# A decoder block: the late modulation products on VectorE, and attention with its TensorE order written out

## The chip, the cores and the metric

One core of one Trainium2 chip runs the whole block. Its engines have a queue each and are tied together by semaphores: TensorE (PE) multiplies matrices into PSUM, VectorE (DVE), ScalarE (ACT) and GpSimd (POOL) do the elementwise work, and DMAs are issued from the queues of SyncE (SP) and ACT. The metric is the device time of one execution in microseconds (us); smaller is better. Of the kernel before three runs were timed, and one more execution was profiled.

## The reference

The input x is 1024 tokens of 1024 channels, with one conditioning vector c. All is float32.

```python
mod = silu(c) @ w_ada + b_ada                    # 6 x 1024: sh1, sc1, g1, sh2, sc2, g2
h = rmsnorm(x, norm1_g) * (1 + sc1) + sh1
u, q, k, v, gate_a, gate_b = split(h @ w_in)     # 512, 512, 512, 512, 1024, 1024
y_a = s5_branch(u, ...) @ w_a                    # 32 groups, 64 complex states each, then a GLU
y_b = stick_breaking_attention(q, k, v) @ w_b    # 8 heads of 64
x = x + g1 * ((sigmoid(gate_a) * y_a + sigmoid(gate_b) * y_b) @ w_o)
h = rmsnorm(x, norm2_g) * (1 + sc2) + sh2
x = x + g2 * ((silu(h @ w_ffn_gate) * (h @ w_ffn_up)) @ w_ffn_down)
out = rmsnorm(x, norm_f_g)
```

Stick-breaking attention gives key j the weight exp(log_sigmoid(z_j) + the sum of log_sigmoid(-z) over the later keys before the query), for keys strictly before the query. So each query needs a running sum over its keys from the latest backwards.

## The kernel before

A scheduler with a timeline of its own sets the order of the instructions on each engine; the program text gives dependencies, buffer counts and a few extra order edges ("pins").

Most products are float32 made of three products of rounded halves: an operand is split into a high half (fp32r, "wh", "pa" first part) and a low half ("wl"), and PE multiplies high x high, high x low, low x high. One projection of 128 output channels is 2 halves of the tokens x 8 slices of channels x 3 = 48 matmuls of 512 columns (`project`, recorded at L619). Its weight is loaded (`weight`, L404), split on ACT or POOL (L411, L413) and DVE or POOL (L414).

The stages, in order: the first modulations and u; the S5 branch in four runs m = 0 to 3 (tables on POOL, scans on DVE, transposes and products on PE, tiles through memory); during it v (`v_proj`) and the first gate (`gate(0, m)`) as filling for PE; then glu, q and k of the first head pair, branch a; then attention; then branch b, the output projection and the feed-forward part.

**The later modulations.** In the S5 stage `ada_rest` makes modulations 4 to 11, two per S5 run: the weight tile `aw` (128 x 2 x 512, 0.5 MB) comes by DMA, PE multiplies it by the conditioning vector into a PSUM bank `adp` (L770, with 32 partitions for every one of four slices), ACT copies the bank to `acc` (L785), and SP stores that (L786). The sum over partitions is made later. The `aw` tiles and `acc` lie in a pool (`ar`) that closes at the end of the S5 stage; tiles of glu (`raw`, loaded at L831) take that place.

**Attention.** There are 4 head pairs, 2 halves Q of the queries, and in each half units of keys: two or one blocks of 128 keys on the diagonal, then one block after the other backwards; 3 units in the first half and 7 in the second, 40 units in all. A unit holds both heads. `scores` makes z = k q on PE (L704) into two PSUM banks, adds the mask on DVE (L712) or copies z (L714), makes log(1 + exp(-|z|)) on ACT (L715 to L717), adds max(z, 0) on DVE (L718), and splits that into halves (high on ACT L719, low on DVE L720). `heads` then subtracts the sums of the units behind it (tile `wb`) on POOL (L737), sums over the keys of the block with triangular ones on PE (L741, PSUM pair `acc`), adds the first row of these sums to the running row on DVE (L750, L752), sends the row to memory (L754) and back to all partitions as the next `wb` (L756), subtracts the sums on DVE (L758), takes exp on ACT (L759), and multiplies by the values on PE (L763). PSUM has eight banks of 512: two pairs for z, one pair for `acc`, one for the values, and one for projections (`mm`).

Beside attention run the projections that nothing in it waits for at once: q and k of the next head pair (`qk_proj`), bound to the scores ten units back, and the eight parts of the second gate (`gate(1, m)`), each bound to one of the scores by the list PINS.

## Time and profile before

| | |
|---|---|
| three timed runs | 1606.18, 1602.16, 1599.55 us; median 1602.16 |
| the profiled execution, its own time | 1606.37 us |
| its span, first to last instruction | 1604.7 us |
| mean granted PE clock | 0.962 |
| S5 stage (v to glu's first matmul) | 101.3 to 316.2 us |
| glu, q and k, branch a | 316.2 to 403.4 us |
| attention (first scores to the start of branch b) | 408.2 to 740.1 us |

In the profile PE is the matmul engine, DVE, ACT and POOL are VectorE, ScalarE and GpSimd; a "q" behind an engine (SPq) means its queue. L and a number is a line of the kernel. A group line gives line, engine, operation, out<-in with sizes, xcount, then busy us, mean ns of one, and the idle time of its engine just before them with what ended most of it. A line of waits gives the total, how many times and the longest. PE matmuls overlap, so the time of one is read from the distance to the next and not from its own length.

### The profile page before, as it was taken

What the parts mean: (1) busy time and instruction counts of PE and PEld (TensorE: products, weight loads), DVE (VectorE), ACT (ScalarE), POOL (GpSimd) and SP (SyncE); (2) the same over time, 40 slices, a digit from 0 to 9 for tenths busy, and PEclk for the clock granted to TensorE, in tenths of its full rate; (3) what the DMA queues carried; (4) which work ended last, traced back from release to release, by engine and by line L of the source; (5) the groups of instructions that cost most, each with busy time, mean ns of one, the idle gap of its engine ahead of it and who ended that gap; (6) DMA issues with size and microseconds to landing.
All of it is one profiled execution on the core that took longest, in us unless ns stands there. A gap on an engine that the chain in (4) does not pass through costs nothing.

```text
span 1604.7 us, 18605 instructions
## 1 busy us (share of the span) xinstructions
PE 1461.0 (91%) x6706; PEld 1118.6 (70%) x6706; DVE 1064.4 (66%) x1269; ACT 640.3 (40%) x824; POOL 768.8 (48%) x602
## 2 busy tenths in 40 slices
...
GB/s 288 157 146 168 170 193 213 157 77 191 79 79 66 119 86 150 71 116 190 151 158 105 129 43 112 109 112 114 116 114 110 64 160 245 146 150 164 99 27 105
DMA packets 180452, 210.48 MB, mean 131 GB/s; under 512 B 28612, under 2 KB 121896, under 8 KB 180360
## 3 DMA queue, kind: packets, MB, share of 16 engines
...
q8 instruction: 53, 0.87, 0.2%
...
## 4 chain that ended last, share of the span: by engine, by line
PE 50%; DVE 19%; POOL 11%; issue 11%; DMA 5%; ACT 4%; SPq 0%; ACTq 0%; DVEq 0%; POOLq 0%
PE tq L1052 10%; PE mm L619 10%; PE wo L1052 8%; PE wo L933 5%; PE ga L619 4%; PE gu L1052 3%; PE mm L578 2%; PE mx L619 2%; PE acc L741 1%; PE z L704 1%; POOL p L71 1%; DVE f L1127 1%; POOL pb L1144 1%; DVE wa L758 1%; DVE x L1140 1%
## 5 line engine op out<-in xcount | busy, mean ns | idle before, releaser
L737 POOL TENSOR_TENSOR wa<-wa,wb 128x1024 f32<-128x1024 f32 (+2 forms) x32 | 68.9, 2153 | 164.3 <-DMA wb<-cD 105.2
L430 POOL TENSOR_TENSOR ws<-wb 128x1024 f32<-128x1024 f32 x29 | 73.3, 2527 | 103.9 <-DVE wl L433 58.4
L430 POOL TENSOR_TENSOR wgs<-wb 128x1024 f32<-128x1024 f32 x15 | 37.0, 2468 | 106.4 <-DVE x L433 37.8
L718 DVE SCALAR_TENSOR_TENSOR ws<-wa,ws 128x1024 f32<-128x1024 f32 (+1 forms) x40 | 56.3, 1411 | 30.1 <-ACT ws L717 30.0
L414 POOL TENSOR_TENSOR wl<-ws,wh 128x1024 fp32r<-128x1024 f32 x10 | 26.3, 2638 | 92.5 <-ACT wh L411 92.5
L1105 POOL TENSOR_TENSOR pa<-pa,row 128x1024 f32<-128x1024 f32 x22 | 64.6, 2957 | 1.9 <-DMA pa<-in_w_ffn_down_dram 1.7
L704 PE MATMUL z<-q,k 64*128 64x512 f32 (+3 forms) x192 | 49.5, 594 | 16.4 <-ACT ws L715 8.0
L758 DVE TENSOR_TENSOR wa<-wa,acc 128x512 f32<-128x512 f32 (+1 forms) x80 | 46.6, 620 | 25.1 <-POOL wa L737 22.9
L1043 POOL TENSOR_TENSOR f<-f,f 128x512 f32<-128x512 f32 x30 | 50.1, 1694 | 27.2 <-DVE f L1033 18.6
L619 PE MATMUL mm<-pa,wgh 128*128 128x512 f32 x176 | 57.8, 409 | 3.7 <-POOL wgh L413 3.4
L619 PE MATMUL mm<-pb,wgh 128*128 128x512 f32 x176 | 57.3, 404 | 1.9 <-ACT gst L657 1.9
L759 ACT ACTIVATE wa<-wa 128x1024 f32<-128x1024 f32 (+1 forms) x40 | 38.8, 970 | 46.0 <-DVE wa L758 46.0
L411 ACT CAST wh<-ws 128x1024 fp32r<-128x1024 f32 x30 | 31.3, 1046 | 62.9 <-PE wo L933 31.2
L413 POOL TENSOR_SCALAR wgh<-wgs 128x1024 fp32r<-128x1024 f32 x8 | 11.5, 1439 | 91.9 <-PE ga L619 59.2
L719 ACT CAST wh<-ws 128x1024 fp32r<-128x1024 f32 (+1 forms) x40 | 38.4, 961 | 42.1 <-DVE ws L718 36.0
L619 PE MATMUL mm<-pa,wh 128*128 128x512 f32 x160 | 51.8, 405 | 0.0
L720 DVE TENSOR_TENSOR wl<-ws,wh 128x1024 fp32r<-128x1024 f32 (+1 forms) x40 | 50.1, 1254 | 2.4 <-ACT wh L719 2.3
L1032 ACT ACTIVATE f<-f 128x1024 f32<-128x1024 f32 x22 | 23.3, 1061 | 62.2 <-DVE f L1072 32.8
L1125 POOL TENSOR_TENSOR wb<-pa 128x512 f32<-128x512 f32 x23 | 40.6, 1776 | 15.7 <-DVE wxl L1123 5.5
L619 PE MATMUL mm<-pb,wh 128*128 128x512 f32 x144 | 45.8, 398 | 1.7 <-ACT q L672 1.7
L741 PE MATMUL acc<-wh,upto 128*128 128x512 f32 (+1 forms) x80 | 34.1, 426 | 13.8 <-DVE wa L758 13.8
L619 PEld LDWEIGHTS mm<-pa,wgh 128*128 128x128 f32 x176 | 34.3, 198 | 17.6 <-POOL wgh L413 5.7
(779 smaller groups left out, 4839.0 us busy)
## 6 DMA issues: line engine op xcount, KB each, us to landing
...
```

The lines of the kernel that those rows point to most:

```text
L430: (add or nc.gpsimd).tensor_tensor(st, a, b, op)
L619: self.nc.tensor.matmul(ps, lhsT=w[a][:, k], rhs=act[h][k][:, b], start=(j == 0), stop=(j == n - 1))
L704: prev = nc.tensor.matmul(z[:, x, f:f + w], lhsT=k[h, P * kb:P * kb + P], rhs=q[h, 512 * Q + c:512 * Q + 512], start=True, stop=True)
L718: nc.vector.scalar_tensor_tensor(st, at, 0.0, st, ALU.max, ALU.add)
L720: nc.vector.tensor_tensor(lt, st, ht.bitcast(F32), ALU.subtract)
L737: nc.gpsimd.tensor_tensor(a[:, :, o], a[:, :, o], behind[:, :, old], ALU.subtract)
L741: nc.tensor.matmul(r[:, x, 0:f], lhsT=self.upto, rhs=parts[n][:, x, 0:f], start=n == 0, stop=n == 1 and behind is not None)
L758: nc.vector.tensor_tensor(a[:, x, 0:f], a[:, x, 0:f], r[:, x, 0:f], ALU.subtract)
L933: nc.tensor.matmul(ps, lhsT=mg[t // 4][k][:, a, P * (t % 4):P * (t % 4) + P], rhs=ws[k // 2][b][:, k % 2], start=(j == 0), stop=(j == 23))
L1043: nc.gpsimd.tensor_tensor(o, a, b, op)
L1052: self.nc.tensor.matmul(ps, lhsT=w[x][:, q, k], rhs=self.B[i](y, k), start=(j == 0), stop=(j == 11))
L1105: nc.gpsimd.tensor_tensor(w, w, g2, ALU.mult)
```

## The change

Two parts.

1. `ada_rest` makes the products on DVE: one multiply and seven multiply-adds of 128 x 512 for each modulation, straight into `acc`. The bank `adp`, PE's products and ACT's copy fall away; the freed bank goes to the projections of that stage (`mx` has 2).

2. Attention is written as one loop over the 40 units in which every PE instruction keeps its program order (`pinned`). At step i come: the sums of unit i, 8 projection matmuls, the values of unit i - 1, the scores of unit i + 3, 8 projection matmuls. The 14 projections (q and k of three head pairs, 8 gates) are one stream of 672 matmuls from a generator, with weights loaded two jobs ahead. PSUM: one pair for z, one pair for `acc`, one bank for the values, three for projections. The copy of z goes from DVE to ACT, the high half from ACT to POOL, the scores' tile `wa` has 5 buffers, and the broadcast row `wb` has 1 where it had 2.

```diff
-ZPB = 2
+ZPB, MXB = 1, 2
-WAB2, WSB, WHB, RWB, CBB = 4, 2, 2, 2, 2
-QPIN = -10
-PINS = (0, 5, 10, 15, 20, 25, 30, 35)
+WAB2, WSB, WHB, RWB, CBB = 5, 2, 2, 2, 1
+LOOK = 3
+FILL = (8, 8, 12)
+JOBS = (("q", 1), ("k", 1), ("g", 0), ("g", 1), ("q", 2), ("k", 2), ("g", 2), ("q", 3), ("k", 3), ("g", 3), ("g", 4), ("g", 5), ("g", 6), ("g", 7))
+AHEAD = 2
...
+    def pinned(self, *args, **kw):
+        return self.tc.keep_in_program_order(self.nc.tensor.matmul(*args, **kw))
+    def fillers(self, qk, qp, kp, gp):
+        nc = self.nc
+        rings = [self.wring[0], self.wring[0], self.wring[2]]
+        jobs = [(n, i) for n, i in JOBS]
+        loaded = []
+        def load(j):
+            n, i = jobs[j]
+            c0 = {"q": 512, "k": 1024, "g": 3072}[n] + P * i
+            loaded.append(self.w3(self.weight(self.in_cols(c0), lo_eng=nc.gpsimd, hi_eng=nc.gpsimd if n == "g" else None, ring=rings[j % 3])))
+        for j in range(AHEAD):
+            load(j)
+        for j, (n, i) in enumerate(jobs):
+            if j + AHEAD < len(jobs):
+                load(j + AHEAD)
...
+            for h in range(2):
+                s = slice(512 * h, 512 * h + 512)
+                ps = self.mm.tile([P, 512], F32, name="mm")
+                c = 0
+                for k in range(KT):
+                    for a, b in PRODUCTS:
+                        self.pinned(ps, lhsT=loaded[j][a][:, k], rhs=self.hT[h][k][:, b], start=c == 0, stop=c == 23)
...
+                        yield
...
     def scores(...)
-            nc.vector.tensor_copy(at, z)
-        nc.scalar.activation(st, at if diag else z, AF.Abs)
+            nc.scalar.copy(a, z)
+        nc.scalar.activation(st, a, AF.Abs)
...
-        nc.scalar.copy(ht, st)
+        nc.gpsimd.tensor_scalar(ht, st, 1.0, 0.0, ALU.mult, ALU.add)
...
+    def attention(self, qk, qp, kp, vp, op, gp, work):
...
+        for i in range(-LOOK, len(units) + 1):
+            if 0 <= i < len(units):
+                self.sums(units[i], work)
+                some(FILL[0])
+            if i > 0:
+                u = units[i - 1]
...
+                self.values(u, ops[u.hp])
+            if i + LOOK < len(units):
+                self.scores(units[i + LOOK], qk, work)
+                some(FILL[1] if i >= 0 else FILL[2])
+        some(10000)
...
-    def ada_rest(self, n, ap, pp, first):
+    def ada_rest(self, n, ap, first):
...
+        acc = ap.tile([P, 512], F32, name="acc", bufs=2)
         for k in range(0, KT, AK):
             w = ap.tile([P, AK, 512], F32, name="aw", bufs=ARB)
             self.after(nc.sync.dma_start(out=w, in_=w_v[:, k:k + AK, 512 * n:512 * n + 512]), first)
-            ws.append(w)
-        ps = pp.tile([P, 512], F32, name="adp")
-        for k in range(KT):
-            self.ada_mm(ps, k, ws[k // AK][:, k % AK])
-        acc = ap.tile([P, 512], F32, name="acc", bufs=2)
-        nc.scalar.copy(acc, ps)
+            for j in range(AK):
+                cj = self.cond[:, k + j:k + j + 1]
+                if k + j == 0:
+                    nc.vector.tensor_scalar(acc, w[:, j], cj, None, ALU.mult)
+                else:
+                    nc.vector.scalar_tensor_tensor(acc, w[:, j], cj, acc, ALU.mult, ALU.add)
         nc.sync.dma_start(out=self.aD[:, n - 4], in_=acc)
```

`sums` and `values` hold what `heads` did behind the scores, in the same form.

The order on the engines, at three places. First DVE in the last S5 run, before (`rt` is a table of S5, `s5s` the injected states, `tc` and `tn` rotations, `scr` scratch, `wl` a weight's low half):

```order
L266 TENSOR_TENSOR rt<-rt,dd 16x8x16
L296 TENSOR_TENSOR scr<-s5s_1786,tc 128x512
L297 TENSOR_TENSOR scr<-s5s_1795,tn 128x512
L298 TENSOR_TENSOR scr<-scr 128x512
L299 TENSOR_TENSOR scr<-s5s_1795,tc 128x512
L300 TENSOR_TENSOR scr<-s5s_1786,tn 128x512
L304 SCALAR_TENSOR_TENSOR scr<-rho,scr 128x128 x4
```

And the same place now (L871 is the new multiply-add):

```order
L871 SCALAR_TENSOR_TENSOR acc<-aw,cond,acc 128x512 x3
L266 TENSOR_TENSOR rt<-rt,dd 16x8x16
L296 TENSOR_TENSOR scr<-s5s_1771,tc 128x512
L871 SCALAR_TENSOR_TENSOR acc<-aw,cond,acc 128x512
L297 TENSOR_TENSOR scr<-s5s_1780,tn 128x512
L871 SCALAR_TENSOR_TENSOR acc<-aw,cond,acc 128x512
L298 TENSOR_TENSOR scr<-scr 128x512
L871 SCALAR_TENSOR_TENSOR acc<-aw,cond,acc 128x512
L299 TENSOR_TENSOR scr<-s5s_1780,tc 128x512
```

The products stand between the steps of S5's chain on the same queue.

Second, SP's queue at the end of S5, before (`yD` is S5's result, `aw` and `aD` the modulations, `raw` glu's input):

```order
L332 DMA yD<-y 16x8x128 x4
L779 DMA aw<-in_w_ada_dram 128x2x512 x2
L658 DMA gD<-gst 128x512
L404 DMA ws<-in_w_glu_dram 128x4x256
L658 DMA gD<-gst 128x512 x2
L786 DMA aD<-acc 128x512
L404 DMA wgs<-in_w_a_dram 128x4x256
L831 DMA raw<-yD 128x512 x2
```

And now:

```order
L872 DMA aD<-acc 128x512
L666 DMA gD<-gst 128x512
L412 DMA ws<-in_w_in_dram 128x8x128
L666 DMA gD<-gst 128x512
L412 DMA wgs<-in_w_in_dram 128x8x128
L412 DMA ws<-in_w_glu_dram 128x4x256
L332 DMA yD<-y 16x8x128 x4
L412 DMA ws<-in_w_glu_dram 128x4x256
L917 DMA raw<-yD 128x512 x2
```

The last modulation is now stored ahead of S5's last result, and the loads of `raw` follow that result.

Third, DVE in attention in a stretch of full units, before (L758 subtracts the sums of one unit, L718 and L720 are the softplus add and low half of a later one):

```order
L720 TENSOR_TENSOR wl_4239<-ws_4237,wh_4238 128x1024
L714 COPY wa_4296<-z_4300 128x1024
L752 TENSOR_TENSOR row_4226<-row_4196,acc_4221 1x1024
L758 TENSOR_TENSOR wa_4206<-wa_4206,acc_4221 128x512 x2
L718 SCALAR_TENSOR_TENSOR ws_4267<-wa_4266,ws_4267 128x1024
L752 TENSOR_TENSOR row_4256<-row_4226,acc_4251 1x1024
L712 TENSOR_TENSOR wa_4444<-z_4448,mask_3566 128x2x384
L718 SCALAR_TENSOR_TENSOR ws_4297<-wa_4296,ws_4297 128x1024
L720 TENSOR_TENSOR wl_4269<-ws_4267,wh_4268 128x1024
```

And now (L796 row, L802 subtraction, L769 add, L771 low half):

```order
L769 SCALAR_TENSOR_TENSOR ws_4930<-wa_4929,ws_4930 128x1024
L771 TENSOR_TENSOR wl_4932<-ws_4930,wh_4931 128x1024
L796 TENSOR_TENSOR row_5011<-row_4965,acc_5006 1x1024
L802 TENSOR_TENSOR wa_4879<-wa_4879,acc_5006 128x512 x2
L769 SCALAR_TENSOR_TENSOR ws_4984<-wa_4983,ws_4984 128x1024
L771 TENSOR_TENSOR wl_4986<-ws_4984,wh_4985 128x1024
L796 TENSOR_TENSOR row_5061<-row_5011,acc_5056 1x1024
```

The order was a changing mixture of units; now it repeats in every full unit, and the low half of a unit follows directly on its add. Between the two, POOL makes the high half (L770).

166 lines of the change are left out of this document (94 added, 72 removed).

## The prediction, made before the changed kernel was run

> **What bounds the kernel now.** I read the page's engine line first, then busy time by stage, then who made TensorE (PE) wait, then the rows of the two stages that the change touches.
>
> ```profile
> PE 1461.0 (91%) x6706; PEld 1118.6 (70%) x6706; DVE 1064.4 (66%) x1269; ACT 640.3 (40%) x824; POOL 768.8 (48%) x602
> ```
>
> PE is busy for 91% of the span. The stages say where the other 9% lie:
>
> ```profile
> core 0: us, PE busy (x) PEld busy (x) DVE busy (x) ACT busy (x) POOL busy (x), PEclk, DMA share, GB/s
> 101.30:316.20 214.90, 204.94 (x1249) 153.98 (x1248) 104.43 (x135) 51.98 (x74) 114.45 (x264) 0.99 0.67 185
> 316.20:403.40 87.20, 87.20 (x385) 71.90 (x383) 31.68 (x39) 28.44 (x41) 6.82 (x8) 1.00 0.44 139
> ...
> 408.20:740.10 331.90, 292.89 (x1203) 181.05 (x1204) 236.29 (x250) 214.46 (x239) 120.32 (x67) 0.93 0.30 98
> ```
>
> From 101 to 316 us (the state-space branch S5 with v and the first gates as filling) PE idles 10.0 us; from 316 to 403 (glu, q/k, branch a) never. In attention, 408 to 740, it idles 39.0 us and the granted clock is 0.93. Who makes it wait there (us in total, times, longest):
>
> ```profile
> PE acc L741 <- DVE wa L758: 13.8, 8, 3.3
> PE z L704 <- ACT ws L715: 8.0, 6, 2.4
> PE z L704 <- DVE wa L712: 3.6, 1, 3.6
> PE mm L619 <- POOL wgh L413: 3.4, 3, 1.4
> PE mm L619 <- POOL wgl L414: 3.2, 3, 2.5
> ```
>
> The column sums wait for their PSUM pair, the scores for theirs, the projections for weights: PE stands with no filler ready. Each such gap costs twice:
>
> ```profile
> 583.90:587.30 3.40, 1.73 (x8) 0.87 (x8) 2.40 (x4) 1.89 (x2) 1.67 (x3) 0.99 0.39 149
> 587.30:590.70 3.40, 3.40 (x9) 0.72 (x6) 3.40 (x5) 2.67 (x4) 2.55 (x1) 0.50 0.06 16
> ```
>
> A stretch with 1.67 us idle out of 3.40 is followed by one at half clock. In 331.9 us a clock of 0.93 loses 0.07 x 331.9 = 23 us. So this stage is bound by order and waits, with PE's work as the floor under it.
>
> The Trainium skill, "TensorE: Matmul & The Clock Gate", section "Why this matters for your kernels", asks for no idle gaps over some 3 us. Here 1.67 us were enough, so the rows decide; by the page the 5 us that I set below for halved stretches would be nothing.
>
> **Attention.** The change removes 16 VectorE (DVE) copies of the scores (they go to ScalarE, ACT) and 40 ACT casts (they go to GpSimd, POOL); it moves all 672 projection matmuls into fixed slots, 16 to a unit, and emits scores three units ahead. PE's floor first:
>
> ```profile
> 289.17 10.88 PE mm L619 x48
> ```
>
> That is 10.88 / 48 = 0.227 us for 512 columns. Projections: 672 x 0.227 = 152 us. Scores are 4,608 columns a head pair (twice 384 + 384 + 512, and four 512); with two heads, two passes and four pairs 73,728 columns, 144 x 0.227 = 33; values as many, 33; sums as many and 4,096 more, 35. Together 252. Before, the stage took 331.9 and left the last 48 projection matmuls for 10.9 more: 343. The 48 are what its groups lack of 672 (the first of eight, which have 112, 112, 56, 56, 96, 96, 48 and 48):
>
> ```profile
> L619 PE MATMUL mm<-pa,wgh 128*128 128x512 f32 x112 | 37.8, 419 | 3.7 <-POOL wgh L413 3.4 <-DVE gst L655 0.4
> ```
>
> What the new order waits for is the chain from unit to unit. Rows of one such chain before:
>
> ```profile
> 479.19 1.27 DVE L758 TENSOR_TENSOR wa<-wa,acc 128x512 f32<-128x512 f32 x2
> 479.29 0.24 SPq L754 DMA_DIRECT2D cD<-row  x1
> 480.39 1.21 DVE L718 SCALAR_TENSOR_TENSOR ws<-wa,ws 128x1024 f32<-128x1024 f32 x1
> 480.56 0.33 SPq L756 DMA_DIRECT2D wb<-cD  x1
> 484.47 2.38 POOL L737 TENSOR_TENSOR wa<-wa,wb 128x1024 f32<-128x1024 f32 x1 [6.98 <-DMA wb<-cD]
> 487.58 1.20 DVE L752 TENSOR_TENSOR row<-row,acc 1x1024 f32<-1x1024 f32 x1
> 482.71 1.23 DVE L720 TENSOR_TENSOR wl<-ws,wh 128x1024 fp32r<-128x1024 f32 x1 [0.25 <-ACT wh L719]
> ```
>
> In the new DVE order a full unit is: row, two subtractions, the softplus add two units ahead, its low half, next row. The low half waits for the high half, now on POOL. The nearest rows for that:
>
> ```profile
> L413 POOL TENSOR_SCALAR wgh<-wgs 128x1024 fp32r<-128x1024 f32 x1 | 1.0, 1044 | 59.2 <-PE ga L619 59.2
> L413 POOL TENSOR_SCALAR wgh<-wgs 128x1024 fp32r<-128x1024 f32 x6 | 9.4, 1569 | 19.9 <-issue 19.9
> L414 POOL TENSOR_TENSOR wl<-ws,wh 128x1024 fp32r<-128x1024 f32 x6 | 16.8, 2803 | 3.4 <-ACT wh L411 3.4
> ```
>
> 1.04 us in a stage with little DVE work, 1.57 in attention; I take 1.57. The loop goes round in two units: subtractions 1.27, add 1.21, high half 1.57, low half 1.23, row 1.20, row to POOL's start by two DMAs 484.47 - 479.29 = 5.2, POOL's subtraction 2.38, and six hand-overs of 0.1 (480.56 against 479.19 + 1.27): 14.7, or **7.3 us a full unit**. With the short high half it is 7.1. The halved broadcast buffer adds nothing here: the read waits for POOL's subtraction, but that loop is 480.56 to 484.47 = 3.9, and 2.4, so 6.3 us. PE's own slots in a full unit are 16 + 4 + 4 + 4 matmuls, 28 x 0.227 = 6.35. ACT's four activations and the copy, at 1.06 (the row below), are 5.3; they hide in 7.3, and if that cover went, the values would come late by the difference. On SP's queue weight loads and gate stores now stand between some units' row write and broadcast; each costs 0.3 us of issue there, and more if it waits for its tile, with the broadcast queued behind it: that belongs to the upper end.
>
> ```profile
> L759 ACT ACTIVATE wa<-wa 128x1024 f32<-128x1024 f32 x24 | 25.3, 1055 | 37.3 <-DVE wa L758 37.3
> ```
>
> Of 40 units, 16 are full ones beside full ones (7.3), 8 diagonal ones are 512 wide (PE's 6.35) and 16 are 384 wide (16 x 0.227 + 12 x 0.17 = 5.7): 117 + 51 + 91 = 259. Ahead stand 36 fillers and three scores, 10.5; behind, the last chain, its values and 20 fillers, also about 10.5. POOL makes 14 weight low halves at 2.8; a quarter of them in the path is 10. Three halved stretches at 1.7 are 5. Sum 295, against 343: **-48 us**. Ends: PE's floor with both ends, 273 (-70); every step of the loop at contended values (rival D), 380 (+37).
>
> **S5 stage.** The change removes 32.8 us of PE and adds 64 DVE products of 128x512 with both tensors in SBUF:
>
> ```profile
> L770 PE MATMUL adp<-aw,cond 128*32 128x512 f32 x128 | 32.8, 604 | 0.1
> L298 DVE TENSOR_TENSOR scr<-scr 128x512 f32<-128x512 f32 x4 | 2.8, 692 | 0.2
> L414 DVE TENSOR_TENSOR wl<-ws,wh 128x1024 fp32r<-128x1024 f32 x9 | 17.4, 1937 | 3.8 <-ACT wh L411 3.6
> L414 DVE TENSOR_TENSOR wgl<-wgs,wgh 128x1024 fp32r<-128x1024 f32 x5 | 6.1, 1216 | 5.9 <-ACT wgh L411 5.9
> ```
>
> 64 x 0.69 = 44 us on a DVE that is busy 104 of 215 us, so there is room in sum; but DVE runs in order, and a product that waits for its weights (or for POOL) holds the S5 step behind it. In this stage the same form took 1.94 where it takes 1.22 elsewhere, so up to 64 x 1.1 = 70.
>
> The Trainium skill, "SBUF — State Buffer", section "Who interferes with whom", says that a DVE instruction with two SBUF inputs contends with a GpSimd one that reads SBUF, and that the later one blocks fully. The trace agrees in kind (1.94 against 1.22); by that rule the products fall among POOL's tables and slow S5, which is rival B.
>
> What PE saves counts only as far as S5 ends in time, for glu waits for it:
>
> ```profile
> L329 ACT COPY y<-s5a x8: 585/585/587, 150.3 to 267.4; 128x512 f32<-128x512 f32 x8
> L831 SPq DMA_DIRECT2D raw<-yD x8: 319/319/425, 287.8 to 303.6; - x8
> L820 DVE TENSOR_TENSOR yp<-y,yp x4: 1224/1226/1227, 295.7 to 309.7; 128x1024 fp32r<-128x1024 f32 x4
> L619 PE MATMUL ga<-yp,wh x64: 388/389/390, 316.2 to 337.5; 128*128 128x512 f32 x64
> ```
>
> y is done at 268, its stores at about 275, but the loads of raw start at 287.8, behind the last modulation on SP's queue; the operands are ready at 310.9 and PE comes to glu at 316. In the change raw follows the stores: from 268, stores 7, loads 15.8, and 310.9 - 303.6 = 7.3 make 298, 18 earlier, if S5 keeps its time. PE's floor is 316 - 33 = 283. By the new order only 96 matmuls (22 us) follow the last S5 product as filling, so PE idles some 9 us there. The 32 weight tiles of 0.5 MB must now come sooner (DMA share 0.67), and where one is late DVE waits in order. Taking S5 8 us later, a fifth of the 44 us of products, since most fall into DVE's idle half: **-10 us** (between -33, and +25 if most of the products' time fell into S5's chain). From glu on PE was full, so what is won stays.
>
> **Sum.** -48 - 10 = -58 on a profiled 1606.4 us (span 1604.7 and 1.7 around it): 1548. The runs' median is 1602.2, 4.2 below that execution; against it the same sum gives **1544 us**. Branch b and the rest have the same work; I cost them at nothing, since their loads are issued during attention (DMA share 0.30).
>
> **Rivals.**
> A, PE's floor: if DMA and POOL are quicker than the rows above, attention takes 273 and S5 gives 25: 1602 - 70 - 25 = 1507. For it: fillers stand at every wait. Against: the 7.3 loop lies above 6.35.
> B, the products delay S5: at the contended rate they take 64 x 0.69 x 1.94 / 1.22 = 70 us, and with half of that in front of S5's steps it ends 35 late, 35 - 18 = 17 after now: 1602 - 48 + 17 = 1571. For it: the 1.94 us row; against: DVE is half idle there.
> C, no effect: the waits only move, 343 again, S5 -5: 1597. Against it: 39 us of idle and 23 of clock have causes that the order removes.
> D, slower: the in-order chain of DVE and POOL takes over as the bound. Place: the low half on DVE waiting for POOL's high half while POOL is in a 2.8 us weight half or waits for the broadcast. With the longest add 2.4, low half 1.5, high half and subtraction 2.8 each (POOL's contended form above) and DMAs of 6, a full unit takes 9 us (1.3 + 2.4 + 2.8 + 1.5 + 1.2 + 6 + 2.8, by two), the narrower ones with the same two DMAs some 8.3, 8.6 on average: 344 + 36 for ends and conversions, so +37, less 10: 1629.
>
> ```profile
> 485.22 2.44 DVE L718 SCALAR_TENSOR_TENSOR ws<-wa,ws 128x768 f32<-128x768 f32 x1 [1.28 <-ACT ws L717]
> L720 DVE TENSOR_TENSOR wl<-ws,wh 128x1024 fp32r<-128x1024 f32 x24 | 35.0, 1460 | 1.3 <-ACT wh L719 1.3
> ```
>
> D decides from 7.9 us on average (343 - 36 + 10, by 40).
>
> **Numbers.** Forecast 0.53, A 0.19, B 0.15, C 0.05, D 0.08. The range runs from 1510 to 1588: A's end to somewhat above B, leaving C and D out. About 0.5% (8 us) is what a measurement here can tell from no change. Faster 0.87 (forecast, A, B), same 0.05 (C), slower 0.08 (D).
>
> **What would show it.** In the trace of the changed kernel: PE's idle time in attention under 25 us, clock above 0.97; scores to the last filler in 295 us; POOL's subtractions 7.3 us apart in a run of full units; the waits of PE named after DVE's subtraction, no longer after ACT. In S5: glu's first matmul 5 to 20 us earlier, with PE idle before it. Wrong if full units come 8 us apart or more, or glu starts after 316.

## The result

| | before | after |
|---|---|---|
| median of the timed runs | 1600.9 us (4 runs) | 1583.6 us (4 runs) |
| ratio, 95% interval | | 0.9887 (0.9865 to 0.991) |
| span of the profiled execution | 1604.7 us | 1582.1 us |
| S5 stage until glu's first matmul | 101.3 to 316.2 us | 101.3 to 314.9 us |
| glu, q and k, branch a | to 403.4 us | to 407.2 us |
| attention: first scores to the last projection matmul; before, first scores to branch b (331.9) and 10.9 for the 48 projection matmuls left over | 343 us | 317.7 us |

The change is faster by 1.1%, 17 us, where 57 were forecast. The parts below are read from the two profiled executions, which lie 22.6 us apart: the one of the kernel before took 5.5 us more than the median of its timed runs. Attention gave 25 us instead of 48. The products on DVE gave nothing: branch a ends 3.8 us later than before, and the first scores are 0.6 us later (408.8 against 408.2). The rest of the program lost some 2 us.

The page's engine line and the busy time by stage, with the same columns as before (time, then busy us and instructions of PE, PEld, DVE, ACT, POOL, then clock, DMA share, GB/s):

```profile
PE 1424.0 (90%) x6578; PEld 1117.5 (71%) x6578; DVE 1094.8 (69%) x1317; ACT 616.2 (39%) x792; POOL 821.3 (52%) x642
```

```profile
101.30:314.90 213.60, 180.64 (x1122) 158.20 (x1121) 146.33 (x197) 42.00 (x60) 134.71 (x264) 0.93 0.67 184
...
408.80:726.50 317.70, 288.38 (x1251) 182.90 (x1252) 227.39 (x233) 191.84 (x212) 149.49 (x107) 0.97 0.30 98
```

PE is busy 37 us less, and still for only 90% of the span. The S5 stage is nearly as long as before, with 33.0 us of idle PE (213.60 - 180.64; 10.0 before) and a clock of 0.93 (0.99 before). Attention keeps 29.3 us of idle time (39.0 before) and a clock of 0.97. What PE waits for, in attention and then in the S5 stage (total, times, longest):

```profile
PE acc L701 <- DVE wa L802: 26.2, 19, 5.8
...
PE s5a L236 <- POOL scr L75: 20.1, 4, 7.2
PE s5a L327 <- DVE h L319: 7.9, 2, 6.6
```

In attention nearly all waiting of PE now has one name: the sums wait until DVE's subtraction has freed their only PSUM pair. In the S5 stage PE waits for S5's own chain over POOL and DVE.

**One slow pair of units.** The lines below are from the timeline of the changed kernel (start, duration, engine, line, idle time before in brackets). L802 is the subtraction of the sums, L769 the softplus add, L770 and L771 its high and low half, L796 the running row, L798 and L800 the two DMAs of the broadcast row, L781 POOL's subtraction of it, L422 a weight's low half:

```profile
475.10 2.39 POOL L422 TENSOR_TENSOR wgl<-wgs,wgh 128x1024 fp32r<-128x1024 f32 x1
...
475.18 1.28 DVE L802 TENSOR_TENSOR wa<-wa,acc 128x512 f32<-128x512 f32 x2 [0.88 <-POOL wa L781]
...
476.38 2.19 DVE L769 SCALAR_TENSOR_TENSOR ws<-wa,ws 128x1024 f32<-128x1024 f32 x1
...
478.76 1.05 POOL L770 TENSOR_SCALAR wh<-ws 128x1024 fp32r<-128x1024 f32 x1 [1.27 <-PE mm L701]
...
479.77 2.38 POOL L781 TENSOR_TENSOR wa<-wa,wb 128x1024 f32<-128x1024 f32 x1
479.85 3.38 DVE L771 TENSOR_TENSOR wl<-ws,wh 128x1024 fp32r<-128x1024 f32 x1 [0.41 <-POOL wh L770]
...
483.15 1.20 DVE L796 TENSOR_TENSOR row<-row,acc 1x1024 f32<-1x1024 f32 x1
484.38 0.24 SPq L798 DMA_DIRECT2D cD<-row  x1
...
485.65 0.32 SPq L800 DMA_DIRECT2D wb<-cD  x1
...
489.26 2.36 POOL L781 TENSOR_TENSOR wa<-wa,wb 128x1024 f32<-128x1024 f32 x1 [1.82 <-DMA wb<-cD]
...
491.66 0.69 DVE L802 TENSOR_TENSOR wa<-wa,acc 128x512 f32<-128x512 f32 x1 [3.23 <-PE mx L701]
```

From one L802 to the one two units later go 491.66 - 475.18 = 16.5 us, 8.2 a unit. (From the first sums of a full unit to those of the next unit go 8.4 us on the mean of 15.) The steps are those of the forecast's loop. But the add takes 2.19 us beside POOL's L422, and the low half 3.38 beside POOL's subtraction, which starts 0.08 us before it; alone they take 1.21 and 1.23. In all of this stage the 30 full-size adds and low halves with no such POOL instruction beside them take 1.20 to 1.23 us, the 18 with one 1.23 to 3.40. The low half ends 1.08 us after POOL's instruction does (483.23 against 482.15), and the add 1.08 us after L422: DVE stands until POOL is done. The row, behind the low half on DVE, comes that much later.

This agrees with the Trainium skill, "SBUF — State Buffer", section "Who interferes with whom": a DVE instruction with two SBUF inputs contends with a GpSimd one that reads SBUF, and the later one is blocked fully.

### The profile page after: what moved, and what is told of

It is laid out like the page before. It is cut to its first block, busy times and chain, and to the rows that moved or that the text cites. A ratio compares the mean times of both kernels' runs of the same rounds, so it can differ in the third digit from the quotient of the medians.

```text
span 1582.1 us, 18396 instructions
## 1 busy us (share of the span) xinstructions
PE 1424.0 (90%) x6578; PEld 1117.5 (71%) x6578; DVE 1094.8 (69%) x1317; ACT 616.2 (39%) x792; POOL 821.3 (52%) x642
## 4 chain that ended last, share of the span: by engine, by line
PE 30%; DVE 10%; issue 5%; POOL 4%; ACT 1%; DMA 1%; POOLq 0%; DVEq 0%; ACTq 0%
PE tq L1138 11%; PE wo L1138 9%; PE wo L1019 5%; PE gu L1138 3%; POOL pa L1191 1%; DVE f L1213 1%; POOL wb L1211 1%; POOL pb L1230 1%; DVE pb L1226 1%; DVE x L1226 1%; DVE f L1209 1%; DVE wl L1209 1%; DMA pa<-in_w_ffn_down_dram 1%; DVE ft L438 1%; PE tq L1220 0%
## 5 line engine op out<-in xcount | busy, mean ns | idle before, releaser
L438 POOL TENSOR_TENSOR ws<-wb 128x1024 f32<-128x1024 f32 x29 | 73.2, 2524 | 105.7 <-DVE wl L441 59.9
L770 POOL TENSOR_SCALAR wh<-ws 128x1024 fp32r<-128x1024 f32 (+1 forms) x40 | 38.6, 964 | 124.7 <-DVE ws L769 87.9
L422 POOL TENSOR_TENSOR wl<-ws,wh 128x1024 fp32r<-128x1024 f32 x14 | 37.1, 2656 | 116.3 <-ACT wh L419 106.9
L771 DVE TENSOR_TENSOR wl<-ws,wh 128x1024 fp32r<-128x1024 f32 (+1 forms) x40 | 66.1, 1653 | 36.8 <-POOL wh L770 36.7
L781 POOL TENSOR_TENSOR wa<-wa,wb 128x1024 f32<-128x1024 f32 (+2 forms) x32 | 67.8, 2120 | 31.8 <-DMA wb<-cD 26.1
L802 DVE TENSOR_TENSOR wa<-wa,acc 128x512 f32<-128x512 f32 (+1 forms) x80 | 46.8, 623 | 29.9 <-POOL wa L781 26.7
L871 DVE SCALAR_TENSOR_TENSOR acc<-aw,cond,acc 128x512 f32<-128x512 f32 x56 | 54.7, 978 | 18.1 <-DMA aw<-in_w_ada_dram 17.5
L769 DVE SCALAR_TENSOR_TENSOR ws<-wa,ws 128x1024 f32<-128x1024 f32 (+1 forms) x40 | 53.4, 1336 | 16.4 <-ACT ws L768 16.3
L701 PE MATMUL acc<-wh,upto 128*128 128x512 f32 (+1 forms) x80 | 32.7, 409 | 26.9 <-DVE wa L802 26.2
L766 ACT ACTIVATE ws<-wa 128x1024 f32<-128x1024 f32 (+1 forms) x40 | 38.9, 973 | 37.3 <-DVE wa L763 36.6
L701 PE MATMUL z<-q,k 64*128 64x512 f32 (+3 forms) x192 | 41.8, 526 | 3.3 <-DVE wa L763 1.7
L701 PEld LDWEIGHTS acc<-wh,upto 128*128 128x128 f32 x80 | 15.5, 194 | 37.9 <-issue 29.7
L1129 POOL TENSOR_TENSOR f<-f 128x512 f32<-128x512 f32 x20 | 42.2, 2126 | 0.0
L1220 PE MATMUL tq<-f,f 128*128 128x512 f32 x96 | 31.1, 407 | 11.8 <-DVE f L1213 11.8
L1220 PE MATMUL wo<-f,f 128*128 128x512 f32 x132 | 40.7, 389 | 0.0
```

The source lines that it names most:

```text
L438: (add or nc.gpsimd).tensor_tensor(st, a, b, op)
L701: return self.tc.keep_in_program_order(self.nc.tensor.matmul(*args, **kw))
L769: nc.vector.scalar_tensor_tensor(st, a, 0.0, st, ALU.max, ALU.add)
L771: nc.vector.tensor_tensor(lt, st, ht.bitcast(F32), ALU.subtract)
L781: nc.gpsimd.tensor_tensor(a[:, :, o], a[:, :, o], g.behind[:, :, old], ALU.subtract)
L871: nc.vector.scalar_tensor_tensor(acc, w[:, j], cj, acc, ALU.mult, ALU.add)
```

## The experiments

Attention runs from the first scores to the end of the last projection matmul in the profiled execution. A ratio is to the kernel before, timed beside it; where none is given there was one timed execution. "PE products" means that the modulations' products are on TensorE as before.

| run | what differs | attention, us | time, us | ratio (95%) |
|---|---|---|---|---|
| changed kernel | | 317.7 | 1583.6 | 0.9887 (0.9865 to 0.991) |
| products_only | kernel before, products on DVE | | 1601.5 | 1.0009 (0.9996 to 1.0023) |
| narrow_products | changed, products of 8 columns, the rest left out | 317.7 | 1573.7 | |
| attention_only | changed, PE products | 317.7 | 1579.2 | 0.9874 (0.9859 to 0.9888) |
| high_on_act | changed, high half on ACT | 317.1 | 1576.6 | 0.985 (0.9833 to 0.9866) |
| narrow_subtraction | changed, POOL's subtraction of 8 columns, the rest left out | 279.4 | 1543.2 | |
| single_input | changed, two one-input POOL instructions instead of the subtraction, which is left out | 316.0 | 1579.1 | |
| off_chain | narrow_subtraction, and behind it a full-size POOL addition whose result is not used | 297.7 | 1561.0 | |
| row_on_tensor | PE products, PE adds the row | 363.6 | 1625.4 | 1.0146 (1.0125 to 1.0168) |
| two_row_tiles | PE products, two broadcast tiles | 320.8 | 1580.2 | 0.9853 (0.9831 to 0.9875) |
| sums_first | PE products, subtractions exchanged | 312.0 | 1573.0 | 0.9821 (0.9788 to 0.9854) |
| sums_first_act | sums_first, high half on ACT | 312.6 | 1574.0 | 0.9836 (0.9806 to 0.9867) |
| late_values | sums_first, values a unit later, scores a unit later | 367.7 | 1631.1 | 1.0187 (1.0165 to 1.0209) |
| late_values_act | late_values, high half on ACT | 328.9 | 1590.3 | 0.9917 (0.9893 to 0.9942) |
| late_values_wide | sums_first, values a unit later, six score tiles | 313.1 | 1575.9 | 0.9823 (0.9794 to 0.9853) |
| late_values_wide_act | the same, high half on ACT | 312.3 | 1572.5 | 0.9815 (0.9783 to 0.9847) |
| only_all_dve | attention_only, row's subtraction on DVE | 313.9 | 1575.7 | 0.9839 (0.9813 to 0.9866) |
| exchanged_all_dve | sums_first, row's subtraction on DVE | 284.4 | **1546.8** | 0.9667 (0.9643 to 0.969) |
| wide_all_dve | late_values_wide, row's subtraction on DVE | 285.2 | 1547.5 | 0.9666 (0.9639 to 0.9694) |

### The two parts apart

attention_only: the changed kernel with `ada_rest` and its PSUM bank as in the kernel before.

```diff
...
-                    nc.vector.scalar_tensor_tensor(acc, w[:, j], cj, acc, ALU.mult, ALU.add)
...
+            self.ada_mm(ps, k, ws[k // AK][:, k % AK])
...
+        nc.scalar.copy(acc, ps)
...
```

> The new attention with the modulations' products left on TensorE, as in the kernel before. Theory: the products on VectorE cost about 4 us in all (branch a ends 3.6 us later in the changed kernel than before), and the whole gain is attention's 25. Then glu's first matmul stays at about 316 us, attention takes about 318 us to its last filler, and the time is 1601 - 25 = 1576 to 1580, some 4 below the changed kernel. Rival: the products gained their 10 us as forecast and attention gave only 7; then this kernel takes about 1594.

products_only: the kernel before with the new `ada_rest`, the same lines the other way round.

> The kernel before with the products on VectorE, attention untouched. Theory: the 33 us that TensorE is spared turn into idle time and half clock in the same stage, since S5 itself ends some 24 us later behind the products; branch a ends 3 to 6 us later than before, and the time is 1603 to 1607. The forecast's S5 step, as rival: 10 us less, 1591.

1579.2 and 1601.5 us. The products have no effect that can be measured (0.9996 to 1.0023; the expected 1603 to 1607 were too high); all that the change wins comes from attention. The forecast's rival numbers, 1594 and 1591, fall. The mechanism is in the trace of the changed kernel, first by tiles (count, min/median/max ns, first and last start), then by groups of instructions:

```profile
L329 ACT COPY y<-s5a x8: 586/586/588, 156.0 to 291.1; 128x512 f32<-128x512 f32 x8
L917 SPq DMA_DIRECT2D raw<-yD x8: 319/320/426, 296.4 to 315.4; - x8
L627 PE MATMUL ga<-yp,wh x64: 389/389/632, 315.0 to 341.3; 128*128 128x512 f32 x64
```

```profile
L871 DVE SCALAR_TENSOR_TENSOR acc<-aw,cond,acc 128x512 f32<-128x512 f32 x56 | 54.7, 978 | 18.1 <-DMA aw<-in_w_ada_dram 17.5
L869 DVE TENSOR_SCALAR acc<-aw,cond 128x512 f32<-128x512 f32 x8 | 6.1, 767 | 8.2 <-DMA aw<-in_w_ada_dram 8.1 <-DMA u<-uD 0.2
```

S5's last y comes at 291.1 where it came at 267.4. So the loads of raw start 8.6 us later than before although they now stand right behind the stores, and glu starts 1.2 us earlier, with gaps (the first ga matmuls run from 315.0 to 341.3, 26.3 us; before 316.2 to 337.5, 21.3). From S5's last y to glu 48.8 us became 23.9 (316.2 - 267.4, 315.0 - 291.1): what the new order of the queue won there, S5's delay of 24 us took. Of PE's 32.8 us of saved work 23 became idle time (33.0 - 10.0), and 8.5 went into slower matmuls: PE's busy time fell only by 24.3 us (204.94 to 180.64), at a mean clock of 0.93 instead of 0.99. The stage became 1.3 us shorter.

### What holds S5: narrow_products

```diff
-                    nc.vector.scalar_tensor_tensor(acc, w[:, j], cj, acc, ALU.mult, ALU.add)
+                    nc.vector.scalar_tensor_tensor(acc[:, 0:8], w[:, j, 0:8], cj, acc[:, 0:8], ALU.mult, ALU.add)
```

> The changed kernel with 56 of the 64 products on VectorE cut to 8 columns (the modulations are so left out of the other columns from the second slice on); the weights are loaded as before. Theory one, the products' own time and their contention hold S5: y is done near 268 us again instead of 291, glu's first matmul comes at 298 to 305, branch a ends 8 to 12 us sooner, 1570 to 1575. Theory two, what holds S5 is that VectorE waits in order for the modulations' weights, so y stays at 285 or later, glu's first matmul at 313 or later, 1580 or more.

Its y by tile, its products by groups, and its S5 stage as a window:

```profile
L329 ACT COPY y<-s5a x8: 585/586/589, 162.3 to 279.3; 128x512 f32<-128x512 f32 x8
```

```profile
L871 DVE SCALAR_TENSOR_TENSOR acc<-aw,cond,acc 128x8 f32<-128x8 f32 x56 | 30.4, 545 | 43.2 <-DMA aw<-in_w_ada_dram 42.4 <-DVE acc L871 0.2
```

```profile
101.30:309.50 208.20, 179.63 (x1129) 156.17 (x1128) 120.60 (x198) 44.89 (x64) 115.90 (x268) 0.96 0.68 190
```

y ends at 279.3, half way between 267.4 and 291.1, glu's first matmul comes at 309.5, and the one execution took 1573.7: the time is that of theory one, the places lie between the two. So 12 of the 24 us by which S5 is later go when the columns are left out; POOL's busy time falls with them, from 134.7 to 115.9, near the 114.5 of the kernel before. The other 12 stay, and the run does not show why. DVE stands 42.4 us for the modulations' weights, with S5's steps behind it, as theory two has it. But the products' time is not gone either. Their median is 0.23 us (0.75 in the changed kernel), yet two of them take 6.4 and 6.8 us, which makes the mean of 0.545. Here is one, merged with the short one after it, and the last of the 128x256 instructions on POOL beside it:

```profile
127.67 7.08 DVE L871 SCALAR_TENSOR_TENSOR acc<-aw,cond,acc 128x8 f32<-128x8 f32 x2 [3.51 <-DMA aw<-in_w_ada_dram]
...
133.73 0.73 POOL L76 TENSOR_TENSOR tn<-tn,p 128x256 f32<-128x256 f32 x1
```

All that time POOL makes a table of S5 with two-input instructions that follow each other without a gap, and the product (127.67 to 134.48) ends as the last of them does (134.46). In the changed kernel one product takes 6.7 us in such a place. So the collision with POOL is in both kernels, and the scheduler placed the narrow products differently: how the 24 us divide stays open.

### Attention: is it the subtraction on POOL?

Four kernels each change one thing about POOL's share. high_on_act, whose edit the kernels with "_act" in their names have too:

```diff
-        nc.gpsimd.tensor_scalar(ht, st, 1.0, 0.0, ALU.mult, ALU.add)
+        nc.scalar.copy(ht, st)
```

> The changed kernel with the high half of the weights' logarithm back on ScalarE. Theory of the collision: on GpSimd the high half stands just ahead of the subtraction of the broadcast row, so the low half on VectorE and that subtraction start together; the low half then takes 3.4 us instead of 1.23 and the next row stands behind it. With the high half on ScalarE the two come apart: low half 1.3 to 1.45 us on the mean instead of 1.65, full units at about 7.5 us instead of 8.2, attention about 300 instead of 318, the time 1565 to 1572. Rival: what sets the pace is the length of the chain alone; the high half is as long on ScalarE (1.06), so nothing changes, 1584, or ScalarE with six instructions of 1.06 a unit becomes the bound and it is slower, 1590.

Attention 317.1: no change. (The 7 us between the medians of the two kernels are not in attention, and the two intervals meet; I make nothing of them.) The collision was put down to the queue order "high half, then subtraction" on POOL, and that is refuted. The low half became shorter (58.5 us for the 40, 1.46 each), but the two still meet, now when the broadcast lands. narrow_subtraction:

```diff
-            nc.gpsimd.tensor_tensor(a[:, :, o], a[:, :, o], g.behind[:, :, old], ALU.subtract)
+            nc.gpsimd.tensor_tensor(a[:, :, o][:, :, 0:8], a[:, :, o][:, :, 0:8], g.behind[:, :, old][:, :, 0:8], ALU.subtract)
```

> The changed kernel with GpSimd's subtraction of the broadcast row cut to 8 columns of a head (the sums of the units behind are so left out of all but these). Collision theory: the low half on VectorE falls from 1.65 to about 1.3 us on the mean, its 3.4 us cases vanish, and TensorE's wait for the sums' PSUM pair falls from 26 to under 8 us: attention about 290. Rival, length of the chain alone: the loop loses the subtraction's 2.2 us in two units (40 units by 1.1 is at most 44, but TensorE's 279 us of work at full clock stops it), and the low halves stay at 1.65, since they would be slow for another reason (the weights' low halves on GpSimd).

Attention as a window, then low half and add by groups:

```profile
405.80:685.20 279.40, 276.00 (x1251) 179.68 (x1252) 202.34 (x233) 193.19 (x212) 91.78 (x107) 1.00 0.34 111
```

```profile
L771 DVE TENSOR_TENSOR wl<-ws,wh 128x1024 fp32r<-128x1024 f32 (+1 forms) x40 | 46.4, 1160 | 34.6 <-POOL wh L770 34.5
L769 DVE SCALAR_TENSOR_TENSOR ws<-wa,ws 128x1024 f32<-128x1024 f32 (+1 forms) x40 | 47.0, 1174 | 13.1 <-ACT ws L768 12.9
```

279.4 us, PE busy for 276.0 of them at full clock. That is PE's real floor in this stage, and nearly the whole loss against it, 38 us, hangs on one 2.4 us instruction. The same two lines in the changed kernel:

```profile
L771 DVE TENSOR_TENSOR wl<-ws,wh 128x1024 fp32r<-128x1024 f32 (+1 forms) x40 | 66.1, 1653 | 36.8 <-POOL wh L770 36.7
L769 DVE SCALAR_TENSOR_TENSOR ws<-wa,ws 128x1024 f32<-128x1024 f32 (+1 forms) x40 | 53.4, 1336 | 16.4 <-ACT ws L768 16.3
```

Together 26 us more of DVE time for the same 80 instructions. But the subtraction is also 2.4 us in the chain. To part the two, single_input was to keep its length with one-input instructions, and off_chain keeps a full two-input instruction out of the chain:

```diff
-            nc.gpsimd.tensor_tensor(a[:, :, o], a[:, :, o], g.behind[:, :, old], ALU.subtract)
+            for _ in range(2):
+                nc.gpsimd.tensor_scalar(a[:, :, o], g.behind[:, :, old], -1.0, 0.0, ALU.mult, ALU.add)
```

> The changed kernel with GpSimd's subtraction (2.38 us, two inputs) replaced by two instructions on the broadcast row alone (one input each, two times 1.05 us), so that the chain stays nearly as long but no GpSimd instruction of two inputs stands in it; the scores themselves are left out of the exponent. Collision theory: the low half falls to about 1.2 us on the mean and the add to 1.2, TensorE waits under 12 us for the sums' pair, and attention takes 280 to 295. Chain-length theory: with 2.1 of the 2.38 us still in the loop, attention stays at 310 to 318.

```diff
-            nc.gpsimd.tensor_tensor(a[:, :, o], a[:, :, o], g.behind[:, :, old], ALU.subtract)
+            nc.gpsimd.tensor_tensor(a[:, :, o][:, :, 0:8], a[:, :, o][:, :, 0:8], g.behind[:, :, old][:, :, 0:8], ALU.subtract)
+            nc.gpsimd.tensor_tensor(g.behind[:, :, old], g.behind[:, :, old], g.behind[:, :, old], ALU.add)
```

> The changed kernel with GpSimd's subtraction cut to 8 columns of a head, as in the narrow subtraction, and behind it a full-size two-input instruction on GpSimd that nothing on VectorE waits for (an addition of the broadcast row to itself; the sums behind are left out of all but 8 columns). Collision theory: low half and add are slow again, 1.5 to 1.65 and 1.3 us on the mean, and attention takes 300 to 318. Chain-length theory: what counts is that the subtraction is out of the loop, so attention stays at 280 to 285, although the low half is slow in places.

The low half in single_input, then in off_chain:

```profile
L771 DVE TENSOR_TENSOR wl<-ws,wh 128x1024 fp32r<-128x1024 f32 (+1 forms) x40 | 54.5, 1362 | 26.3 <-POOL wh L770 26.2
```

```profile
L771 DVE TENSOR_TENSOR wl<-ws,wh 128x1024 fp32r<-128x1024 f32 (+1 forms) x40 | 52.0, 1299 | 42.7 <-POOL wh L770 42.6
```

Two places in single_input:

```profile
461.78 3.03 POOL L782 TENSOR_SCALAR wa<-wb 128x1024 f32<-128x1024 f32 x2
...
461.85 2.06 DVE L771 TENSOR_TENSOR wl<-ws,wh 128x1024 fp32r<-128x1024 f32 x1 [1.25 <-POOL wh L770]
...
622.75 3.27 POOL L782 TENSOR_SCALAR wa<-wb 128x1024 f32<-128x1024 f32 x2
...
622.75 1.23 DVE L771 TENSOR_TENSOR wl<-ws,wh 128x1024 fp32r<-128x1024 f32 x1 [1.24 <-POOL wh L770]
```

single_input, 316.0, looks like a victory of the chain, but it does not part the two theories, for POOL's one-input instructions collide as well. A low half that starts 0.07 us behind the first of them takes 2.06 us. Where it starts at the same time it takes 1.23, and POOL's two take 3.27 together instead of two times 1.05, in the chain. The 40 low halves and 40 adds still took 54.5 + 53.3 = 107.8 us, with 93.4 in narrow_subtraction and 119.5 in the changed kernel. off_chain, 297.7: 20 of the 38 us are won back although POOL has as much to do, and 18 stay, which neither theory had. It has about as much of the collisions (52.0 + 53.6 = 105.6 us), now outside the step from the broadcast to the sums. The 18 us belong to the collisions or to POOL's queue, in which a high half can stand behind the extra instruction. What the length of the chain alone costs is shown by neither run. (In single_input a weight's low half on POOL can also fall between the two instructions; that adds to its chain.)

### Taking the row out of the chain: row_on_tensor

```diff
+                self.pinned(r[:, x, old.start - c.start:f], lhsT=self.ones[0:1], rhs=g.row[:, x, old], start=False, stop=True)
...
-            nc.vector.tensor_tensor(g.row[:, :, c], past[:, :, c], r[0:1, :, fs], ALU.add)
-            nc.sync.dma_start(out=d, in_=g.row.rearrange("p a b -> p (a b)"))
-            nc.sync.dma_start(out=g.behind.rearrange("p a b -> p (a b)"), in_=d[0].partition_broadcast(P))
+            nc.vector.tensor_copy(g.row[:, :, c], r[0:1, :, fs])
```

> The new attention with the products back on TensorE, and the broadcast row taken out: instead of two DMAs and GpSimd's subtraction, TensorE adds the running row to the sums with a matmul of one row of ones (float32, two passes a head), and VectorE only copies the new row. Both theories of attention say the same here: nothing of GpSimd and no DMA is left in the loop, and attention is bound by TensorE: 276 us of work plus 53,248 columns by 0.227 / 512 = 24, about 300, so 1579 - 18 = 1561. If a matmul of one row costs more, or VectorE's copy of the row is waited for in every unit, 1575 to 1590.

363.6 us, a miss by 64 for both theories. The loop is gone: PE never idles. But the stage is 84 us longer than PE's floor (363.6 - 279.4) instead of 24. The timeline, then three windows:

```profile
553.59 1.12 PE L701 MATMUL acc<-row,ones 1*128 1x512 f32 x2
554.64 0.50 PE L701 MATMUL acc<-wh,upto 128*128 128x512 f32 x1
```

```profile
404.50:768.00 363.50, 363.50 (x1379) 203.45 (x1380) 202.44 (x233) 195.75 (x212) 77.39 (x59) 0.95 0.12 40
552.90:556.30 3.40, 3.40 (x10) 1.18 (x8) 1.04 (x2) 3.34 (x4) 2.37 (x1) 1.00 0.00 0
556.30:559.70 3.40, 3.40 (x9) 2.48 (x8) 3.23 (x4) 0.81 (x2) 0.00 (x0) 0.50 0.54 154
```

One head's row of 512 columns takes two passes and 554.64 - 553.59 = 1.05 us, 0.53 a pass where 0.227 was assumed, and the clock falls to 0.50 in places without any idle PE.

### The order of the two subtractions

sums_first subtracts the sums first, on DVE, which frees the PSUM pair; POOL subtracts the broadcast row after that, ahead of the exponential. (In this kernel and those built on it L796 is DVE's subtraction, L800 that of the row, L804 the exponential.)

```diff
-        if g.behind is not None:
-            nc.gpsimd.tensor_tensor(a[:, :, o], a[:, :, o], g.behind[:, :, old], ALU.subtract)
         r = self.accp.tile([P, 2, 512], F32, name="acc")
...
         for x in range(2):
             nc.vector.tensor_tensor(a[:, x, 0:f], a[:, x, 0:f], r[:, x, 0:f], ALU.subtract)
+        if g.behind is not None:
+            nc.gpsimd.tensor_tensor(a[:, :, o], a[:, :, o], g.behind[:, :, old], ALU.subtract)
```

> The new attention with the products on TensorE (attention_only), and the two subtractions exchanged: VectorE first subtracts the sums of the unit itself, which frees the PSUM pair, and GpSimd subtracts the broadcast row afterwards, just ahead of the exponential. Loop theory: in the changed kernel two units take 16.4 us because the PSUM pair is freed only behind subtraction 1.4, add 1.2 to 2.2, high half 1.05, low half 1.2 to 3.4, row 1.2, two DMAs 4.9 and GpSimd's subtraction 2.4; with the exchange the DMAs and the subtraction leave that loop, and what is left goes over GpSimd's queue (subtraction 2.4, high half 1.05, low half 1.2, row 1.2, subtraction 1.4: 7.3 a full unit at most) or over TensorE (6.6). Attention falls from 318 to 280 to 300, the time from 1579 to 1541 to 1561. Rival: the loop is not what paces it, but VectorE's in-order queue with the contended low halves (1.65 us on the mean); then attention stays at 310 or more and the time within 8 us of 1579.

> The same with the high half on ScalarE, so that it does not stand behind GpSimd's subtraction. Loop theory: VectorE's own four steps and the high half, 1.4 + 1.2 + 1.05 + 1.2 + 1.2 and hand-overs, about 6.5 a full unit, lie under TensorE's 6.6, and ScalarE has six instructions of 1.06, 6.4 a unit: attention 278 to 285, the time 1539 to 1546, at or below the one with the high half on GpSimd. Rival: ScalarE, now nearly as full as TensorE, delays the exponentials and with them the values: attention 295 or more and TensorE waits named after ScalarE's exponential.

312.0 and 312.6 us: 5 to 6 us better than attention_only, where the loop theory had at least 18 and 33. The wait moved; in sums_first PE now stands at the values:

```profile
PE mm L701 <- ACT wa L804: 20.3, 15, 5.5
PE acc L701 <- DVE wa L796: 7.5, 6, 2.5
```

late_values gives the values one unit more, with the same tiles, so the scores come only two units ahead:

```diff
-LOOK = 3
+LOOK = 2
-        for i in range(-LOOK, len(units) + 1):
+        for i in range(-LOOK, len(units) + 2):
-            if i > 0:
-                u = units[i - 1]
+            if i > 1:
+                u = units[i - 2]
```

> As sums_first, with the values two units behind the sums and the scores two units ahead (the same 5 tiles for the scores). In sums_first the wait only moved: TensorE waits 20 us for ScalarE's exponential, which comes behind GpSimd's subtraction, and 7.5 us for the sums' pair. Moved-wait theory: with one unit (6.6 us) more until the values, the 20 us vanish, attention falls from 312 to 285 to 298 and the time from 1573 to 1546 to 1560. Rival: the contention between VectorE and GpSimd is the floor under every order, 8 us a full unit, and the wait moves on to the sums' pair or the scores: attention 308 or more, 1568 or more.

> The same with the high half on ScalarE. Moved-wait theory: the high half no longer stands behind GpSimd's subtraction, so the sums' pair is waited for less: attention 280 to 290, the time 1540 to 1552, below the one with the high half on GpSimd. Rival as there: 308 or more, or ScalarE with 6.4 us a unit becomes the bound and TensorE waits are named after it, 300 or more.

367.7 and 328.9: the 20 us are gone and longer waits stand in their place, for the halves of the softplus (late_values):

```profile
PE acc L701 <- POOL wh L770: 36.4, 19, 4.0
PE acc L701 <- DVE wl L771: 21.9, 25, 2.7
```

The scores have to be three units ahead. late_values_wide does that with a sixth score tile, for which the running row is kept in place.

```diff
-WAB2, WSB, WHB, RWB, CBB = 5, 2, 2, 2, 1
+WAB2, WSB, WHB, RWB, CBB = 6, 2, 2, 1, 1
-                nc.vector.tensor_tensor(g.row[:, :, c], past[:, :, c], r[0:1, :, fs], ALU.add)
+                nc.vector.tensor_tensor(g.row[:, :, c], g.row[:, :, c], r[0:1, :, fs], ALU.add)
```

> As sums_first, with the values two units behind the sums and the scores still three units ahead: the scores have 6 tiles, and the room comes from the running row, which is now updated in place (one tile instead of two). In late_values the scores came too late and TensorE waited 58 us for the halves. Moved-wait theory: without that, the 20 us that sums_first waits for the exponential vanish and nothing takes their place: attention 285 to 300, the time 1546 to 1562. Rival, contention between VectorE and GpSimd paces every order: the wait goes to the sums' pair, attention 308 or more, 1569 or more.

> The same with the high half on ScalarE. Moved-wait theory: sums_first_act waits 22.6 us for the exponential and 2.8 for the sums' pair, so here 280 to 292 for attention, 1541 to 1555. Rival: 308 or more, 1569 or more.

313.1 and 312.3: the moved-wait theory falls here. The exponential is hardly waited for any more, the sums' pair is again, and on DVE the add is the slow one (waits and group in late_values_wide_act):

```profile
PE acc L701 <- DVE wa L796: 14.0, 6, 4.2
```

```profile
L769 DVE SCALAR_TENSOR_TENSOR ws<-wa,ws 128x1024 f32<-128x1024 f32 (+1 forms) x40 | 68.2, 1704 | 35.6 <-ACT ws L768 35.5
```

two_row_tiles (two broadcast tiles in attention_only, room again from the row in place) asked whether the single tile has a share:

```diff
-WAB2, WSB, WHB, RWB, CBB = 5, 2, 2, 2, 1
+WAB2, WSB, WHB, RWB, CBB = 5, 2, 2, 1, 2
```

> attention_only with two tiles for the broadcast row, as the kernel before had (the room comes from the running row, updated in place); nothing else is changed. If the single tile costs nothing, as the prediction has it, the time is attention_only's 1579, within 6 us, and attention 318. If the broadcast's read, which with one tile waits for GpSimd's subtraction, is a part of the 16.4 us that two units take, attention falls by 8 to 20 us, 1559 to 1571.

1580.2 us and 320.8: it has none.

### Both at once

wide_all_dve and exchanged_all_dve put the row's subtraction on DVE, behind the exchange:

```diff
-            nc.gpsimd.tensor_tensor(a[:, :, o], a[:, :, o], g.behind[:, :, old], ALU.subtract)
+            nc.vector.tensor_tensor(a[:, :, o], a[:, :, o], g.behind[:, :, old], ALU.subtract)
```

> As late_values_wide, with the subtraction of the broadcast row on VectorE (1.2 us) instead of GpSimd (2.4): GpSimd is left with the high halves (one input) and the weights' low halves. VectorE then has 1.4 + 1.2 + 1.2 + 1.2 + 1.2 = 6.3 us in a full unit, under TensorE's 6.6. Contention theory (what is left in late_values_wide is the 31 us by which add and low half are longer than alone): low half and add fall to 1.2 us on the mean, attention from 312 to 282 to 292, the time from 1574 to 1544 to 1554. Rival, VectorE's queue: it now holds everything in order and waits for the broadcast row in it, so 300 or more, 1562 or more.

> The same without the later values (sums_first with the subtraction of the broadcast row on VectorE). Contention theory: 285 to 297 for attention, since the exponential comes 1.2 us sooner than behind GpSimd but is still used one unit behind the sums: 1548 to 1560. Rival as there: 300 or more, with the wait for the exponential still 15 us or more, 1562 or more.

The same move without the exchange:

> attention_only with the subtraction of the broadcast row on VectorE, without exchanging the two subtractions: the fourth corner beside attention_only (1579), sums_first (1573) and exchanged_all_dve (1547). If the contention alone made the loss, attention comes to 285 to 295 and the time to 1547 to 1557 here too. If the loop matters as well, it stays above: on VectorE's queue the subtraction now stands ahead of the next row and waits for the broadcast of the row before, so row 1.2, two DMAs 4.9, subtraction 1.2 and hand-overs, 7.5 us, go round once a unit: attention 300 to 312, the time 1562 to 1574.

Four corners, attention in us:

| | row's subtraction on POOL | on DVE |
|---|---|---|
| ahead of the sums' subtraction | 317.7 (attention_only) | 313.9 (only_all_dve) |
| behind it | 312.0 (sums_first) | 284.4 (exchanged_all_dve) |

Each alone gives 4 to 6 us, both together 33. PE's waits, the low half and the row's subtraction in only_all_dve, and one of those subtractions with what POOL does beside it; then window, waits, low half and the row's subtraction in exchanged_all_dve:

```profile
PE acc L701 <- DVE wa L802: 17.8, 15, 3.3
```

```profile
L771 DVE TENSOR_TENSOR wl<-ws,wh 128x1024 fp32r<-128x1024 f32 (+1 forms) x40 | 50.8, 1271 | 26.4 <-POOL wh L770 26.2
L781 DVE TENSOR_TENSOR wa<-wa,wb 128x1024 f32<-128x1024 f32 (+2 forms) x32 | 48.4, 1512 | 17.3 <-DMA wb<-cD 17.0
```

```profile
626.09 3.22 POOL L422 TENSOR_TENSOR wl<-ws,wh 128x1024 fp32r<-128x1024 f32 x1
...
627.00 3.40 DVE L781 TENSOR_TENSOR wa<-wa,wb 128x1024 f32<-128x1024 f32 x1
```

```profile
405.00:692.00 287.00, 279.22 (x1257) 181.19 (x1257) 233.28 (x266) 192.70 (x213) 95.48 (x76) 0.99 0.33 110
```

```profile
PE acc L701 <- DVE wa L796: 3.4, 2, 3.2
PE mm L701 <- ACT wa L804: 3.0, 1, 3.0
```

```profile
L771 DVE TENSOR_TENSOR wl<-ws,wh 128x1024 fp32r<-128x1024 f32 (+1 forms) x40 | 49.1, 1228 | 24.7 <-POOL wh L770 24.5
...
L800 DVE TENSOR_TENSOR wa<-wa,wb 128x1024 f32<-128x1024 f32 (+2 forms) x32 | 33.1, 1035 | 8.0 <-DMA wb<-cD 7.7
```

The corners look as if either of two causes, the loop and the collisions, held nearly the whole loss alone. They do not show that, for only_all_dve is not free of collisions. There they moved: low halves and adds are short, but the row's subtractions take 48.4 us instead of 33.1, and four of the 16 full-size ones take 2.80 to 3.40 us, each beside a weight's low half on POOL (L422). Its loop is also another one: the subtraction stands ahead of the next row on the same queue, where DVE stands 17.0 us for the broadcast, so the loop goes round once a unit instead of once in two. It came out above both ranges expected of it. The five kernels in one table (us):

| | low halves + adds on DVE | row's subtraction | attention |
|---|---|---|---|
| late_values_wide_act | 124.8 | 71.9, POOL | 312.3 |
| changed kernel | 119.5 | 67.8, POOL | 317.7 |
| sums_first | 106.1 | 81.0, POOL | 312.0 |
| only_all_dve | 95.0 | 48.4, DVE | 313.9 |
| exchanged_all_dve | 93.9 | 33.1, DVE | 284.4 |

What is shown: late_values_wide_act has the pair freed first, a unit more until the values and no high half behind POOL's subtraction, and still takes 28 us more than exchanged_all_dve, with 31 us more in low halves and adds and PE's longest waits for DVE. So with the collisions most of the loss is there also without the changed kernel's loop. What is not shown is the loop alone: no run has it without collisions. And moving the row's subtraction to DVE also makes it shorter (1.23 us instead of 2.38) and frees POOL's queue; no run parts that from the collisions.

In exchanged_all_dve, with the order exchanged and the collisions nearly gone, PE idles 7.8 us of 287.0, at a clock of 0.99. It takes 1546.8 us, 3.3% less than the kernel before (0.9643 to 0.969), and beats both kernels. The later values and the sixth tile add nothing to it (wide_all_dve 1547.5).

## Why the prediction was wrong

**Attention, forecast -48, measured -25.** For the full units the mechanism was right: the sums' pair, the loop through add, halves, row, two DMAs and POOL's subtraction. Two steps failed: low half and add were priced as if they ran alone, and the 24 other units were put at a floor of PE that is too low. From the first sums of a unit to those of the next (39 distances) go:

| units | forecast, us | measured, us | narrow_subtraction, us |
|---|---|---|---|
| 15 full ones (of 16) | 15 x 7.3 = 110 | 125.8 | 98.5 |
| 8 diagonal, 512 wide | 51 | 57.6 | 52.9 |
| 16 of 384 | 91 | 110.0 | 105.7 |

That is 42 us more than forecast in the units, of which its 10 for conversions and 5 for halved stretches cover 15; ahead of the first sums and behind the last went 24 us, where it had 21 and 7.3 for the last unit. Term by term:

- The add at 1.21 and the low half at 1.23 us: in the pair of units above they took 2.19 and 3.38. Over the stage the 40 low halves took 66.1 us and the adds 53.4, where narrow_subtraction has 46.4 and 47.0. The rule that explains it stood in the prediction, but it priced rivals alone: B in S5, and D's longest add in attention.
- The high half at 1.57 us was too dear: 1.05. Row to POOL's start at 5.2 was 4.9 (489.26 less the row's end, 484.35), and the hand-overs took less than the 0.6 set for them. So 14.7 + 0.98 + 2.15 - 0.52 - 0.3 - 0.5 = 16.5 for two full units, as measured.
- PE's floor of 252 us was 276 (narrow_subtraction). The forecast took 0.227 us for every pass of 512 columns; the four float32 passes of a full unit's scores take 1.06 us, not 0.91 (in the trace before too), those of the values 1.01, and the slots of a unit 6.6 us instead of 6.35 or 5.7: in narrow_subtraction all three kinds take 6.6, since the slots of one unit hold scores and values of its neighbours. This did not bind the full units. But the 384 wide ones the forecast had put at 5.7, and 15 of their 19 us too many are this floor; the rest of the 19, and most of the diagonal ones' 7, are waits that it left out there.
- Halved stretches: 9.5 us by the clock (0.03 x 317.7) instead of 5.
- The 21 us of the two ends count 24 fillers and three scores that the units hold already, some 8 us. This error works against the others.
- "The halved broadcast buffer adds nothing": right (two_row_tiles).

Its test said wrong if full units come 8 us apart or more; they come 8.4 apart. That the waits would be named after DVE's subtraction was right, 26.2 of 29.3 us.

**S5, forecast -10, measured nothing** (products_only 0.9996 to 1.0023). The step that failed is "Taking S5 8 us later, a fifth of the 44 us of products": S5 ended 24 us later. The products took 54.7 + 6.1 = 60.8 us, not 44, DVE stood 25.6 us for their weights with S5's steps behind it, and POOL, which makes the tables, was busy for 134.7 us instead of 114.5. The queue's new order, put at 18 us, gave 25, which hid the error. That PE's saving counts only if S5 ends in time was the right condition.

**The rivals.** B had the right place: products in front of S5's steps, 24 late against its 35. It cost less than B's 17 us, since the operands of glu came 1 us earlier, not later; what was lost showed as gaps and half clock. D named the place of attention's loss, the low half on DVE and POOL's queue, and even bounded the add by a contended 2.44 us row; it took 1.5 for the low half where 3.4 happened, but in every unit, and the mean stayed at 7.5 (39 distances between the first sums at 420.4 and the last at 713.7), under its 7.9. A's 273 us for attention lies near what narrow_subtraction shows to be possible (279), by luck: its floor of 252 is too low by 24, and of the 21 for the ends that it adds the larger part is PE's work that the 252 hold already. exchanged_all_dve comes within 5 us of the 279.

What stays open: how the 38 us between attention_only and narrow_subtraction divide between the collisions and the length of the loop. That most of them stay while the collisions do, also with the loop opened, is shown (late_values_wide_act); what the loop costs without collisions is not. S5's 24 us are not divided either.
